# Four begun blocks at the scan's end, a sum of squares on TensorE and 1.1 convolution steps an item in a two-block model kernel

## Chip, cores and metric

One core of a Trainium2 chip runs the whole program. The metric is the device time of one execution in microseconds; the time before is the median of 3 runs.

## What is computed

The input x is 512 x 1024 (float32). A first block of two layers is followed by a second block of two mixers (cut from the reference; `rms_norm` divides by the root of the mean square):

```python
for l in range(2):                                   # first block
    hn = rms_norm(h, norm_mix_pre[l])
    y_attn, y_conv = dilated_attention(hn), short_conv(hn)
    o = gated_delta_rule(q, k, v, g, beta)           # scan over 8 chunks of 64
    y_gdn = rms_norm(o, norm_w) * silu(gate)
    mix = concatenate([y_attn, y_conv, y_gdn]) @ w_out[l]
    h = h + rms_norm(mix, norm_mix_post[l])
    xa = memory_cross_attention(rms_norm(h, norm_xattn_pre[l]), ...)
    h = h + rms_norm(xa, norm_xattn_post[l])
    f = swiglu_ffn(rms_norm(h, norm_ffn_pre[l]), w_gate_up[l], w_down[l])
    h = h + rms_norm(f, norm_ffn_post[l])
for i in range(2):                                   # second block: even, odd
    sh, sc, g = split(silu(c) @ mod_w[i] + mod_b[i])
    hl = rms_norm(x_lat, norm_g[i]) * (1 + sc) + sh
    x_lat = x_lat + g * mixer_i(hl, h_ctx)
return rms_norm(x_lat, final_g)
```

The even mixer attends over 256 context rows and the 512 rows; the odd one is a 31-tap depthwise convolution beside a neighbourhood attention of 8 heads.

## The kernel before

Activations lie transposed, as 8 chunks of 128 features x 512 positions. h is `hT`; a normalised input is held as a high and a low part (`xh`, `xl`). A weight block is 1024 x 128: `weight` loads it on SP's queue into `wr` (3 buffers), ACT casts it to the high part `wh` (L266) and DVE makes the low part `wl` (L267), 4 buffers each. Every product is three matmuls for each chunk, high by high, low by high, high by low (`mm3`, L293 to L295), summed in PSUM over 8 chunks, so a block is 24 matmuls of 128x512.

The order on each engine is set by a scheduler from the order in which the code issues, with some priorities; each engine then runs its rows in order. To fill TensorE, work is written as generators in `self.fill`, and `pump(n)` takes n steps of the first of them. `begin` starts blocks whose input is not ready as a whole, and `advance` adds the next chunk to each begun block as soon as that chunk of x exists (`gps` gives PSUM tile g for a block, `sps` a tile s for two).

Places that the change touches:
- `gdn_scan` (L834 to L872): the delta rule's scan over 8 chunks c. The begun blocks are the first two of `w_out` (g_2418 and g_2419 in the first layer); chunks 0 to 3 of their input are ready before the scan ends. At c = 7 four calls of `gdn_norm` follow, one for each quarter of the positions: the last O (L838, L855 and an add), its square, the scaling on DVE (L885), a transpose on PE (L888) and the gate. Then four `split` and `advance` (xh L399) bring chunks 4 to 7.
- `residual` (L409): R from the sum of squares (L378 the product with ones, then Ln L380 and Exp L381 on ACT), then for each chunk om x weight x R (L420) and the add into hT (L421). After the second layer's feed-forward, `colstat` forms hT's own sum of squares: squares on ACT (L392), seven adds on DVE (L393), one product with a matrix of ones (L378); then `modnorm` (L1341 to L1343) makes the even mixer's input, chunk by chunk, with three begun blocks.
- `ctx_stream` (L1450): the even mixer's work on the context rows, pumped as a filler through the second layer's feed-forward at RATES[1] = 1.1 steps a place, and on through the residual. Its matmuls are 128x256 (s<-ch,wh) and, at its end, for values of the odd mixer (L325 to L327).
- `odd` (L1671): 32 attention items; after the transposes of each, `steps(CR)` takes CR steps of the long convolution (`conv31`, L1795), each step one tap on DVE for each of four chunks (cu, R), 30 steps in all. DVE also masks and reduces for the softmax (L771, L768) and casts weights (L267). What is left of the convolution is run out when the last head begins (`start(3)`).

```python
        def steps(k):
            nonlocal n
            n += k
            while n >= 1:
                for c in conv:
                    next(c, None)
                n -= 1
```

Of the kernel before, what the change touches and what calls it, by code (L numbers as in the profile page):

```python
# [12 lines left out]
AF = mybir.ActivationFunctionType  # L13
# [4 lines left out]
D = 1024  # L18
S = 512
CTX = 256  # L20
MEM = 256
KC = D // 128
# [7 lines left out]
TS, TB = 2, 2  # L30
WP, XP = 1, 2
ER, OR = 1, (1.6, 2.1, 2.1, 1.7)
CR = 1.5
XOP = (0, 1)
RATES = (0.7, 1.1)
WR, WH, WL = 3, 4, 4
HA, HB, HD = 0, 0, 0
MP = (0, 0)
# [172 lines left out]
class Net:  # L211
# [128 lines left out]
    def begin(self, aps, extra=0):  # L340
# [7 lines left out]
        for i, ap in enumerate(aps):  # L348
            wh, wl = self.weight(ap)
            self.begun.append(((ap.tensor.name, ap.offset), wh, wl, ps[i]))  # L350

    def advance(self):
        c = self.nbegun
        self.nbegun += 1
        for _, wh, wl, ps in self.begun:
            self.mm3(ps, wh[:, c], wl[:, c], self.xh[:, c], self.xl[:, c], c == 0, c == KC - 1)


    def pump(self, n=1):
# [15 lines left out]
    def rsqrt_of(self, ss, out, scale, epscol, n=512, lhs=None):  # L375
        nc = self.nc
        ps = self.bps()[:, :n]
        nc.tensor.matmul(ps, self.ones if lhs is None else lhs, ss, start=True, stop=True)  # L378
        bias = 0.0 if epscol is None else self.epst[:, epscol:epscol + 1]
        nc.scalar.activation(out, ps, AF.Ln, bias=bias, scale=scale)  # L380
        nc.scalar.activation(out, out, AF.Exp, scale=-0.5)  # L381
        return ps

    def sumsq(self, acc, src, first, t=None):

# [20 lines left out]
        nc.scalar.copy(self.om[:, c], ps)  # L406
        self.sumsq(acc, ps, c == 0)

    def residual(self, acc, post, pre=None, R=None, scale=1.0 / D, epscol=0, chunk=2, aeps=0, keep=False):  # L409
        nc = self.nc  # L410
        Rp = self.R
        self.pump(2)
        with self.hp(HA):
            self.rsqrt_of(acc, Rp, 1.0 / D, aeps)
        self.pump(3)
        for c in range(KC):
            self.pump(chunk)
            t = self.tmp("rt")
            with self.hp(HB):
                nc.vector.scalar_tensor_tensor(t, self.om[:, c], self.sm(post, c), Rp, ALU.mult, ALU.mult)  # L420
                nc.vector.tensor_add(self.hT[:, c], self.hT[:, c], t)  # L421
                if pre is not None:
                    self.last = self.split(self.xh[:, c], self.xl[:, c], self.hT[:, c], self.sm(pre, c))
            if pre is not None:
                self.advance()
        if pre is not None:
            self.prestat(R, scale, epscol, keep)

    def prestat(self, R, scale=1.0 / D, epscol=0, keep=False):
        nc = self.nc  # L430
# [74 lines left out]
    def first(self, dbg=None):  # L505
# [5 lines left out]
        for l in range(2):  # L511
# [15 lines left out]
            else:  # L527
# [4 lines left out]
                with tc.tile_pool(name="ctx", bufs=1) as p:  # L532
                    self.fill = [self.ctx_stream(p)]
                    acc = self.xo_ffn(l, dbg, 1)
                    self.residual(acc, "f_post1", chunk=1, aeps=None)
                    if dbg and dbg(self, f"h3_{l}"): return
                    self.mark("ctxend")
                    R = self.colstat(self.hT, S, self.R)
                    self.pump(2)
                    self.begin([a["ev_in"][c] for c in (4, 0, 5)])  # L540
                    for _ in self.modnorm(0, 0, self.hT, self.xh, self.xl, S, R):
                        self.advance()
                        self.pump()
                    self.drain()
# [277 lines left out]
    def gdn_scan(self, l, p, heads):  # L822
# [3 lines left out]
        for c in range(8):  # L826
# [38 lines left out]
            if c == 7:  # L865
                while len(self.fill) > 3:
                    self.pump()
                for i in range(4):
                    self.gdn_norm(l, O, i, p)
        self.drain()  # L870
        self.mark(f"gdnend{l}")
        for h in range(4):  # L872
            self.split(self.xh[:, 4 + h], self.xl[:, 4 + h], self.om[:, 4 + h])
            self.advance()

    def gdn_norm(self, l, O, i, p):

# [971 lines left out]
```

## Time and profile before

| | |
|---|---|
| median of 3 runs | 2509.55 us (2506.88 to 2512.07) |
| the profiled execution's own time | 2508.96 us |
| its span, first to last instruction | 2507.2 us |
| mean granted TensorE clock | 0.986 |
| TensorE (PE) busy | 2409.2 us, 96% |
| weight loads (PEld) busy | 1960.1 us, 78% |
| VectorE (DVE) busy | 1755.7 us, 70% |
| ScalarE (ACT) busy | 1272.1 us, 51% |
| GpSimd (POOL) busy | 22.6 us, 1% |
| read from HBM | 240.83 MB, 98 GB/s over the span |

Times in the rows count from the span's start. A matmul's record is longer than its share of the engine, since matmuls are pipelined: what one costs is the distance from its start to the next start.

### The profile page before, as it was taken

What the parts mean: (1) busy time and instruction counts of PE and PEld (TensorE: products, weight loads), DVE (VectorE), ACT (ScalarE), POOL (GpSimd) and SP (SyncE); (2) the same over time, 40 slices, a digit from 0 to 9 for tenths busy, and PEclk for the clock granted to TensorE, in tenths of its full rate; (3) what the DMA queues carried; (4) which work ended last, traced back from release to release, by engine and by line L of the source; (5) the groups of instructions that cost most, each with busy time, mean ns of one, the idle gap of its engine ahead of it and who ended that gap; (6) DMA issues with size and microseconds to landing.
All of it is one profiled execution on the core that took longest, in us unless ns stands there. A gap on an engine that the chain in (4) does not pass through costs nothing.

```text
span 2507.2 us, 34818 instructions
## 1 busy us (share of the span) xinstructions
PE 2409.2 (96%) x13036; PEld 1960.1 (78%) x13036; DVE 1755.7 (70%) x3164; ACT 1272.1 (51%) x2371; POOL 22.6 (1%) x57
## 2 busy tenths in 40 slices
PE   8999899989999989998999999999998999999998
PEld 6678688768888766786887678888876888878787
DVE  7887675499984578876755755556566666669975
ACT  5754454444333447544545644445344666545584
POOL 0000000000000000000000000000000000000000
PEclk9999999999999999999999999999999999999999
DMA  5133133237753321331332233233335421333422
GB/s 180 51 86 77 51 118 126 93 115 238 214 174 109 97 83 51 86 77 51 125 120 78 83 97 97 93 100 127 118 116 155 119 64 56 115 101 99 115 77 68
DMA packets 96025, 263.30 MB, mean 105 GB/s; under 512 B 16232, under 2 KB 32232, under 8 KB 94704
## 3 DMA queue, kind: packets, MB, share of 16 engines
q1 hardware_dynamic: 92592, 257.72, 33.8%
q0 software_dynamic: 704, 2.17, 0.5%
q10 hardware_dynamic: 2560, 1.18, 0.3%
q8 instruction: 103, 1.69, 0.3%
q14 instruction: 66, 0.54, 0.1%
HBM read 240.83 MB, written 4.46 MB: 98 GB/s over the span
## 4 chain that ended last, share of the span: by engine, by line
PE 84%; DVE 9%; ACT 3%; DMA 2%; issue 2%; ACTq 0%; DVEq 0%; SPq 0%
PE g L293 19%; PE g L294 18%; PE g L295 18%; PE b L810 3%; PE s L293 3%; PE s L294 3%; PE s L295 3%; PE s L757 2%; PE b L1417 2%; PE b L378 2%; DVE wl L267 1%; DVE mj L1321 1%; PE b L797 1%; DMA mw<-in_mod_t_dram 1%; PE s L855 1%
## 5 line engine op out<-in xcount | busy, mean ns | idle before, releaser
L293 PE MATMUL g<-xh,wh 128*128 128x512 f32 (+1 forms) x1960 | 784.5, 402 | 40.1 <-ACT xh L400 9.1
L295 PE MATMUL g<-xh,wl 128*128 128x512 f32 (+1 forms) x1960 | 775.1, 396 | 6.0 <-DVE wl L267 5.9
L294 PE MATMUL g<-xl,wh 128*128 128x512 f32 (+1 forms) x1960 | 777.2, 397 | 0.0
L266 ACT CAST wh<-wr 128x1024 fp32r<-128x1024 f32 (+4 forms) x422 | 397.7, 945 | 632.5 <-PE g L294 492.7
L267 DVE TENSOR_TENSOR wl<-wr,wh 128x1024 fp32r<-128x1024 f32 (+4 forms) x422 | 458.4, 1089 | 162.6 <-ACT wh L266 156.5
L293 PEld LDWEIGHTS g<-xh,wh 128*128 128x128 f32 x1960 | 371.9, 190 | 128.1 <-ACT xh L400 12.1
L295 PEld LDWEIGHTS g<-xh,wl 128*128 128x128 f32 x1960 | 372.8, 190 | 85.5 <-DVE wl L267 8.0
L294 PEld LDWEIGHTS g<-xl,wh 128*128 128x128 f32 x1960 | 373.3, 190 | 76.0 <-issue 2.4
L293 PE MATMUL g<-yh,wh 128*128 128x512 f32 x352 | 139.8, 398 | 1.8 <-DVE om L1232 1.7
L294 PE MATMUL g<-yl,wh 128*128 128x512 f32 x352 | 138.1, 392 | 0.0
L295 PE MATMUL g<-yh,wl 128*128 128x512 f32 x352 | 137.9, 392 | 0.1
L1321 DVE CUSTOM_DVE_ANT_0 mj<-mw,csb 128x1024 f32<-128x1024 f32 x96 | 117.2, 1221 | 7.1 <-DMA mw<-in_mod_t_dram 6.0
L1232 DVE TENSOR_TENSOR om<-om,g 128x512 f32<-128x512 f32 x80 | 54.9, 686 | 63.6 <-PE g L295 63.2
L810 PE MATMUL b<-ident,P 128*128 128x128 f32 x608 | 96.0, 277 | 0.4 <-ACT P L783 0.3
L817 ACT COPY pt<-b 128x512 f32<-128x512 f32 (+3 forms) x136 | 71.6, 535 | 45.5 <-PE b L810 44.1
L468 ACT ACTIVATE rt<-rt 128x512 f32<-128x512 f32 x76 | 47.9, 631 | 91.6 <-DVE rt L467 90.5
L810 PEld LDWEIGHTS b<-ident,P 128*128 128x128 f32 x608 | 69.7, 141 | 24.0 <-ACT P L783 6.2
L454 DVE TENSOR_TENSOR fg<-g,R 128x512 f32<-128x512 f32 x42 | 29.0, 690 | 81.3 <-PE g L295 77.4
L783 ACT ACTIVATE P<-P,st 128x512 f32<-128x512 f32 (+4 forms) x96 | 65.9, 687 | 39.0 <-DVE st L779 16.7
L757 PE MATMUL s<-K,Q 128*128 128x256 f32 (+2 forms) x384 | 84.8, 338 | 0.0
L393 DVE TENSOR_TENSOR acc<-acc,sq 128x512 f32<-128x512 f32 (+1 forms) x111 | 75.6, 681 | 5.9 <-ACT sq L392 4.1
L293 PEld LDWEIGHTS g<-yh,wh 128*128 128x128 f32 x352 | 66.2, 188 | 17.1 <-issue 2.5
(444 smaller groups left out, 3899.8 us busy)
## 6 DMA issues: line engine op xcount, KB each, us to landing
wr<-in_w_gu_dram SPq DMA_DIRECT2D x88, 512.0 KB
wr<-in_w_in_dram SPq DMA_DIRECT2D x56, 512.0 KB
mw<-in_mod_t_dram SPq DMA_DIRECT2D x48, 512.0 KB
wr<-in_ev_in_dram SPq DMA_DIRECT2D x40, 512.0 KB
wr<-in_od_in_dram SPq DMA_DIRECT2D x32, 512.0 KB
wr<-in_w_down_dram SPq DMA_DIRECT2D x56, 192.0 KB
wr<-in_w_down_dram SPq DMA_DIRECT2D x24, 384.0 KB
wr<-in_w_out_dram SPq DMA_DIRECT2D x16, 512.0 KB
```

The lines of the kernel that those rows point to most:

```text
L266: nc.scalar.copy(hi[:, :k], raw[:, :k])
L267: nc.vector.tensor_sub(lo[:, :k], raw[:, :k], hi[:, :k].bitcast(F32))
L293: mm(ps, wh, xh, start=first, stop=False)
L294: mm(ps, wh, xl, start=False, stop=False)
L295: mm(ps, wl, xh, start=False, stop=last)
L393: nc.vector.tensor_add(acc, acc, t)
L757: self.nc.tensor.matmul(sp[:, c], q, K[u][:, k:k + c.stop - c.start], start=u == 0, stop=u == 1)
L783: nc.scalar.activation(P[:, c], src[i], AF.Exp, bias=shift, scale=-1.0 if neg else 1.0, accum_out=one(3 + i))
L810: nc.tensor.transpose(ps[:, 128 * (j % 4):128 * (j % 4) + 128], P, self.ident)
L817: nc.scalar.copy(out(j - m + 1, m), src)
L1232: nc.vector.tensor_add(self.om[:, c], self.om[:, c], ps)
L1321: nc.vector.tensor_tensor_reduce(out=junk, in0=raw, in1=csb[:, b], scale=1.0, scalar=0.0, op0=ALU.mult, op1=ALU.add, accum_out=self.mod[i] ...
```

## The change

Four edits.
1. In `gdn_scan`, at c = 7, a generator `begin_more` joins the fillers: it begins blocks 2 and 3 of `w_out` in one tile s and issues their chunks 0 to 3. Behind the scan chunks 4 and 5 are split and advanced, 6 and 7 split alone, and `finish` adds what is left to each of the four blocks. Both layers.
2. `residual` has a flag `stat`, set for f_post1 alone: each chunk of hT is squared on ACT as soon as it is added, and a product with the ones adds it up in PSUM (L451, 8 products). `colstat`, with its seven adds, is gone there; `rsqrt_end` is the Ln and Exp alone.
3. RATES[1] goes from 1.1 to 1.07.
4. CR goes from 1.5 to 1.1.

```diff
--- before.py
+++ after.py
@@ -30,9 +30,9 @@
 TS, TB = 2, 2
 WP, XP = 1, 2
 ER, OR = 1, (1.6, 2.1, 2.1, 1.7)
-CR = 1.5
+CR = 1.1
 XOP = (0, 1)
-RATES = (0.7, 1.1)
+RATES = (0.7, 1.07)
 WR, WH, WL = 3, 4, 4
 HA, HB, HD = 0, 0, 0
 MP = (0, 0)
@@ -349,11 +349,30 @@
             wh, wl = self.weight(ap)
             self.begun.append(((ap.tensor.name, ap.offset), wh, wl, ps[i]))
 
+    def begin_more(self, aps):
+
+        p = self.sps()
+        for i, ap in enumerate(aps):
+            wh, wl = self.weight(ap)
+            ps = p[:, 512 * i:512 * i + 512]
+            self.begun.append(((ap.tensor.name, ap.offset), wh, wl, ps))
+            for c in range(self.nbegun):
+                self.mm3(ps, wh[:, c], wl[:, c], self.xh[:, c], self.xl[:, c], c == 0, False)
+                if c % 2:
+                    yield
+
     def advance(self):
         c = self.nbegun
         self.nbegun += 1
         for _, wh, wl, ps in self.begun:
             self.mm3(ps, wh[:, c], wl[:, c], self.xh[:, c], self.xl[:, c], c == 0, c == KC - 1)
+
+    def finish(self):
+
+        for _, wh, wl, ps in self.begun:
+            for c in range(self.nbegun, KC):
+                self.mm3(ps, wh[:, c], wl[:, c], self.xh[:, c], self.xl[:, c], c == 0, c == KC - 1)
+        self.nbegun = KC
 
 
     def pump(self, n=1):
@@ -376,10 +395,14 @@
         nc = self.nc
         ps = self.bps()[:, :n]
         nc.tensor.matmul(ps, self.ones if lhs is None else lhs, ss, start=True, stop=True)
+        self.rsqrt_end(ps, out, scale, epscol)
+        return ps
+
+    def rsqrt_end(self, ps, out, scale, epscol):
+        nc = self.nc
         bias = 0.0 if epscol is None else self.epst[:, epscol:epscol + 1]
         nc.scalar.activation(out, ps, AF.Ln, bias=bias, scale=scale)
         nc.scalar.activation(out, out, AF.Exp, scale=-0.5)
-        return ps
 
     def sumsq(self, acc, src, first, t=None):
 
@@ -406,7 +429,8 @@
         nc.scalar.copy(self.om[:, c], ps)
         self.sumsq(acc, ps, c == 0)
 
-    def residual(self, acc, post, pre=None, R=None, scale=1.0 / D, epscol=0, chunk=2, aeps=0, keep=False):
+    def residual(self, acc, post, pre=None, R=None, scale=1.0 / D, epscol=0, chunk=2, aeps=0, keep=False, stat=False):
+
         nc = self.nc
         Rp = self.R
         self.pump(2)
@@ -419,12 +443,19 @@
             with self.hp(HB):
                 nc.vector.scalar_tensor_tensor(t, self.om[:, c], self.sm(post, c), Rp, ALU.mult, ALU.mult)
                 nc.vector.tensor_add(self.hT[:, c], self.hT[:, c], t)
+                if stat:
+                    sq = self.tmp("sq")
+                    nc.scalar.activation(sq, self.hT[:, c], AF.Square)
+                    if c == 0:
+                        ps = self.bps()
+                    nc.tensor.matmul(ps, self.ones, sq, start=c == 0, stop=c == KC - 1)
                 if pre is not None:
                     self.last = self.split(self.xh[:, c], self.xl[:, c], self.hT[:, c], self.sm(pre, c))
             if pre is not None:
                 self.advance()
         if pre is not None:
             self.prestat(R, scale, epscol, keep)
+        return ps if stat else None
 
     def prestat(self, R, scale=1.0 / D, epscol=0, keep=False):
         nc = self.nc
@@ -532,10 +563,11 @@
                 with tc.tile_pool(name="ctx", bufs=1) as p:
                     self.fill = [self.ctx_stream(p)]
                     acc = self.xo_ffn(l, dbg, 1)
-                    self.residual(acc, "f_post1", chunk=1, aeps=None)
+                    ps = self.residual(acc, "f_post1", chunk=1, aeps=None, stat=True)
                     if dbg and dbg(self, f"h3_{l}"): return
                     self.mark("ctxend")
-                    R = self.colstat(self.hT, S, self.R)
+                    R = self.R
+                    self.rsqrt_end(ps, R, 1.0 / D, 0)
                     self.pump(2)
                     self.begin([a["ev_in"][c] for c in (4, 0, 5)])
                     for _ in self.modnorm(0, 0, self.hT, self.xh, self.xl, S, R):
@@ -865,13 +897,16 @@
             if c == 7:
                 while len(self.fill) > 3:
                     self.pump()
+                self.fill.append(self.begin_more([a["w_out"][l][c] for c in (2, 3)]))
                 for i in range(4):
                     self.gdn_norm(l, O, i, p)
         self.drain()
         self.mark(f"gdnend{l}")
         for h in range(4):
             self.split(self.xh[:, 4 + h], self.xl[:, 4 + h], self.om[:, 4 + h])
-            self.advance()
+            if h < 2:
+                self.advance()
+        self.finish()
 
     def gdn_norm(self, l, O, i, p):
 
```

On PE at the end of the first layer's scan, from its last transposes (b<-ident,O) to the begun blocks (g_2418, g_2419), there stood before:

```order
L888 MATMUL b_2474<-ident,O_2041 128x128 x4
L855 MATMUL s_2402<-vn_2403,at_1050 64x128
L855 MATMUL s_2402<-vn_2403,at_1055 64x128
L855 MATMUL s_2402<-vn_2403,at_1060 64x128
L855 MATMUL s_2402<-vn_2403,at_1065 64x128
L888 MATMUL b_2493<-ident,O_2041 128x128 x4
L888 MATMUL b_2512<-ident,O_2041 128x128 x4
L293 MATMUL g_2418<-xh,wh_2422 128x512
L293 MATMUL g_2419<-xh,wh_2428 128x512
L294 MATMUL g_2418<-xl,wh_2422 128x512
```

and now, with s_2545 the tile of blocks 2 and 3 (line 923 was 888, 887 was 855):

```order
L887 MATMUL s_2402<-vn_2403,at_1065 64x128
L294 MATMUL s_2545<-xl,wh_2548 128x512
L295 MATMUL s_2545<-xh,wl_2549 128x512
L293 MATMUL s_2545<-xh,wh_2548 128x512
L294 MATMUL s_2545<-xl,wh_2548 128x512
L295 MATMUL s_2545<-xh,wl_2549 128x512
L293 MATMUL s_2545<-xh,wh_2566 128x512
L294 MATMUL s_2545<-xl,wh_2566 128x512
L923 MATMUL b_2493<-ident,O_2041 128x128 x4
L295 MATMUL s_2545<-xh,wl_2567 128x512
L293 MATMUL s_2545<-xh,wh_2566 128x512
L294 MATMUL s_2545<-xl,wh_2566 128x512
```

Between those small products, and ahead of the first matmul of g_2418, 24 matmuls into s_2545 now stand, in groups of 7, 7, 8 and 2; before, blocks 2 and 3 (g_2631, g_2670) followed behind g_2418 and g_2419.

On DVE at the end of the second layer's feed-forward residual there stood before, from the last multiply and adds into hT on, with acc the sum of hT's squares:

```order
L420 SCALAR_TENSOR_TENSOR rt_15786<-om,small,R 128x512
L420 SCALAR_TENSOR_TENSOR rt_15795<-om,small,R 128x512
L421 TENSOR_TENSOR hT<-hT,rt_15786 128x512
L421 TENSOR_TENSOR hT<-hT,rt_15795 128x512
L393 TENSOR_TENSOR acc_1545_15798<-acc_1545_15798,sq_15800 128x512
L267 TENSOR_TENSOR wl_15828<-wr_15825,wh_15827 128x1024
L393 TENSOR_TENSOR acc_1545_15798<-acc_1545_15798,sq_15803 128x512
L267 TENSOR_TENSOR wl_15850<-wr_15847,wh_15849 128x1024
L393 TENSOR_TENSOR acc_1545_15798<-acc_1545_15798,sq_15806 128x512
L267 TENSOR_TENSOR wl_15856<-wr_15853,wh_15855 128x1024
```

and now (line 444 was 420, 445 was 421, 422 was 399):

```order
L267 TENSOR_TENSOR wl_15752<-wr_15749,wh_15751 128x1024
L422 TENSOR_TENSOR Kcl_15694<-s_15656,Kch_15693 128x256
L444 SCALAR_TENSOR_TENSOR rt_15761<-om,small,R 128x512
L444 SCALAR_TENSOR_TENSOR rt_15773<-om,small,R 128x512
L445 TENSOR_TENSOR hT<-hT,rt_15761 128x512
L445 TENSOR_TENSOR hT<-hT,rt_15773 128x512
L267 TENSOR_TENSOR wl_15782<-wr_15779,wh_15781 128x1024
L422 TENSOR_TENSOR Kcl_15743<-s_15705,Kch_15742 128x256
L444 SCALAR_TENSOR_TENSOR rt_15791<-om,small,R 128x512
L267 TENSOR_TENSOR wl_15808<-wr_15805,wh_15807 128x1024
L445 TENSOR_TENSOR hT<-hT,rt_15791 128x512
L267 TENSOR_TENSOR wl_15823<-wr_15820,wh_15822 128x1024
```

The seven adds into acc are gone, and the weight casts (L267) that stood between them stand between the adds into hT. PE has a product L451 for each chunk, between the matmuls on context.

On DVE in the odd mixer, this ended the stretch of 47 rows ahead of the cast of wl_20233, with om the convolution's sum:

```order
L1795 SCALAR_TENSOR_TENSOR om<-R,small,om 128x503
L1795 SCALAR_TENSOR_TENSOR om<-cu_19137,small,om 128x503
L471 TENSOR_TENSOR sq_20170<-rt_20168,sq_20170 128x512
L1795 SCALAR_TENSOR_TENSOR om<-cu_19206,small,om 128x503
L1406 TENSOR_TENSOR om<-om,sq_20170 128x512
L1795 SCALAR_TENSOR_TENSOR om<-cu_19275,small,om 128x503
L771 ISA P_20223,st_20222<-s_20200,rpb_20194 128x512
L771 ISA st_20222 128x1
L768 TENSOR_REDUCE st_20222<-s_20200 128x1
L267 TENSOR_TENSOR wl_20233<-wr_20230,wh_20232 128x1024
```

and this now ends the stretch of 29 rows ahead of the same block's cast, wl_20203 (line 1830 was 1795, 803 was 771):

```order
L1830 SCALAR_TENSOR_TENSOR om<-R,small,om 128x510
L1830 SCALAR_TENSOR_TENSOR om<-cu_19135,small,om 128x510
L1830 SCALAR_TENSOR_TENSOR om<-cu_19204,small,om 128x510
L803 ISA P_19894,st_19856<-s_19875,rpb_19705 128x512
L803 ISA st_19856 128x1
L800 TENSOR_REDUCE st_19856<-s_19875 128x1
L1830 SCALAR_TENSOR_TENSOR om<-cu_19273,small,om 128x510
L809 TENSOR_SCALAR st_19856<-st_19856 128x1
L267 TENSOR_TENSOR wl_20203<-wr_20200,wh_20202 128x1024
```

Of the 47 rows 20 are taps of the convolution, of the 29 now 12. Ahead of the cast at the last head (wl_20781) 69 rows now stand behind the cast before it, 28 of them taps.

## Rows read from the trace of the kernel before

**Rows 1.** The page: busy time by engine, and the chain that ended last.

```profile
PE 2409.2 (96%) x13036; PEld 1960.1 (78%) x13036; DVE 1755.7 (70%) x3164; ACT 1272.1 (51%) x2371; POOL 22.6 (1%) x57
...
PE 84%; DVE 9%; ACT 3%; DMA 2%; issue 2%; ACTq 0%; DVEq 0%; SPq 0%
```

**Rows 2.** Busy time by stretch: length, PE, PEld, DVE, ACT, POOL, granted clock, DMA share, GB/s.

```profile
250.00:300.00 50.00, 43.06 (x256) 33.39 (x253) 31.61 (x87) 19.18 (x66) 0.00 (x0) 0.90 0.09 32
...
1450.00:1850.00 400.00, 400.00 (x2122) 333.76 (x2121) 220.32 (x374) 179.13 (x335) 0.00 (x0) 1.00 0.33 105
...
1850.00:1900.00 50.00, 41.87 (x217) 33.37 (x216) 46.35 (x75) 29.17 (x47) 0.00 (x0) 1.00 0.52 157
...
2300.00:2350.00 50.00, 50.00 (x364) 41.73 (x363) 48.81 (x106) 31.71 (x75) 0.00 (x0) 1.00 0.53 143
```

**Rows 3.** PE's timeline, end of the first layer's scan: start, length, instruction, [idle before <-releaser].

```profile
285.32 1.08 PE L855 MATMUL s<-vn,at 64*64 64x128 f32 x8 [1.24 <-ACT O L838]
...
287.93 0.88 PE L888 MATMUL b<-ident,O 128*128 128x128 f32 x4 [1.53 <-DVE O L885]
...
290.47 1.09 PE L888 MATMUL b<-ident,O 128*128 128x128 f32 x4 [1.66 <-DVE O L885]
...
293.17 1.22 PE L293 MATMUL g<-xh,wh 128*128 128x512 f32 x2 [1.62 <-ACT xh L399]
...
307.66 0.59 PE L293 MATMUL g<-xh,wh 128*128 128x512 f32 x1
```

**Rows 4.** PE's timeline, end of the second layer's scan.

```profile
1169.27 1.22 PE L293 MATMUL g<-xh,wh 128*128 128x512 f32 x2 [1.62 <-ACT xh L399]
...
1182.73 0.59 PE L293 MATMUL g<-xh,wh 128*128 128x512 f32 x1
...
1188.40 0.39 PE L293 MATMUL g<-xh,wh 128*128 128x512 f32 x1
```

**Rows 5.** PE's timeline, the second layer's last residual and the even mixer's start.

```profile
1874.47 1.02 PE L378 MATMUL b<-acc,ones 128*128 128x512 f32 x2
...
1890.52 0.50 PE L326 MATMUL s<-wl,ch 128*128 128x512 f32 x1 [1.39 <-DVE wl L267]
...
1894.79 0.50 PE L326 MATMUL s<-wl,ch 128*128 128x512 f32 x1 [1.26 <-DVE wl L267]
...
1902.30 1.74 PE L378 MATMUL b<-acc,ones 128*128 128x512 f32 x2 [4.71 <-DVE acc L393]
...
1907.02 1.22 PE L293 MATMUL g<-xh,wh 128*128 128x512 f32 x2 [2.98 <-ACT xh L1342]
...
1912.73 0.49 PE L294 MATMUL g<-xl,wh 128*128 128x512 f32 x1
...
1926.43 1.12 PE L378 MATMUL b<-sq,blk 128*128 128x512 f32 x2
```

**Rows 6.** The same stretch on DVE and on ACT.

```profile
1891.72 1.28 DVE L421 TENSOR_TENSOR hT<-hT,rt 128x512 f32<-128x512 f32 x2
...
1893.52 1.21 DVE L267 TENSOR_TENSOR wl<-wr,wh 128x1024 fp32r<-128x1024 f32 x1
...
1893.70 0.63 ACT L392 ACTIVATE sq<-hT 128x512 f32<-128x512 f32 x1 [2.53 <-DVE acc L393]
...
1904.08 0.69 ACT L380 ACTIVATE R<-b,epst 128x512 f32<-128x512 f32 x1 [2.49 <-PE b L378]
```

**Rows 7.** The odd mixer, DVE's timeline and then PE's.

```profile
2331.53 1.22 DVE L267 TENSOR_TENSOR wl<-wr,wh 128x1024 fp32r<-128x1024 f32 x1
...
2354.99 1.21 DVE L267 TENSOR_TENSOR wl<-wr,wh 128x1024 fp32r<-128x1024 f32 x1
...
2356.89 2.04 DVE L1795 SCALAR_TENSOR_TENSOR om<-cu,small,om 128x502 f32<-128x502 f32 x3
...
2356.25 0.50 PE L295 MATMUL g<-xh,wl 128*128 128x512 f32 x1 [4.12 <-DVE wl L267]
...
2359.93 0.46 PE L295 MATMUL g<-xh,wl 128*128 128x512 f32 x1
```

## Prediction

> **What bounds the kernel.** I read the page first: TensorE (PE) is busy 2409.2 of the 2507.2 us span, DVE 70%, ACT 51%, and the chain that ended last is 84% PE and 9% DVE [rows 1]. So time leaves in two ways only: PE does less, or one of its holes closes. The table by stage says where holes are. In the first block's second feed-forward part PE is busy for the whole 400.00 us from 1450 to 1850: nothing can be won there. At the end of the first layer's scan it has 43.06 of 50 at a granted clock of 0.90, in 1850 to 1900 only 41.87, while DVE has 46.35 [rows 2]. In 2300 to 2350 PE is full, but so is DVE (48.81) [rows 2]: a DVE instruction that comes late there finds no slack.
>
> Then the holes, in PE's order of time. At the scan's end PE waits four times (1.24, 1.53, 1.66, 1.62 us) in a chain in which ACT and DVE finish the last heads; the first two after it show 1.22 us for the pair [rows 3], which is the 1.2 GHz level and fits the window's granted 0.90. At the 2.4 GHz level they stand 0.23 apart: 24 in 5.67 us from 1182.73 to 1188.40 [rows 4]. Around the end of that feed-forward part PE stands 4.71 us for DVE's last sum of squares, runs the product with ones, stands 2.98 us for the normalised input, and then runs at the slow spacing until 1912.73 [rows 5]. In the last stage it stands 4.12 us for a weight's low half (wl) that DVE makes, then runs slowly until 2359.93, nine matmuls in 3.7 us, 0.41 apart [rows 7].
>
> **1. Four begun blocks in the scan, both layers.** Removed nothing; 24 matmuls (two blocks, chunks 0 to 3) move from behind the scan to between its last products; the order's rows show them in four groups of 7, 7, 8 and 2. Their weights' casts stand at the same places on ACT and DVE, so no other engine gets work. PE's holes there add up to 1.24+1.53+1.66+1.62 = 6.05 us [rows 3], the 24 matmuls are 24 x 0.23 = 5.5 us, so they fit. PE runs in order: where a group is a little longer than its hole, the next small product, and the chain behind it, starts late; I take 0.7 us in all (0.3 to 1.0). After the chain 48 matmuls remain (four blocks, chunks 4 to 7), 11.0 us if the clock stays high, and a ones-product of some 0.45. So the next block starts at 293.17+0.7+11.0+0.45 = 305.3. Before, it started at 307.66+5.67 = 313.3 [rows 3, 4]: **-8.0**. Second layer: 1169.27+0.7+11.0+0.45 = 1181.4 against 1188.40 [rows 4]: **-7.0** (its restart was shorter before: 13.46 us from the chain's end to the last block's start, 14.49 in the first layer [rows 3, 4]). Without any gain in clock it is 5.5 minus at most 1 for the delay, so -4.5 each; with no delay -8.7 and -7.7.
>
> **2. Sum of squares on TensorE, with 3. the slower pump (1.1 to 1.07).** The pump moves some 32 matmuls of 256 columns from ahead of the ffn's last sum (the 1874.47 row) to behind it; counted in the order, 92 in place of 60 stand between that sum and the first begun block. Ahead of it PE is full [rows 2], so the sum comes 32 x 0.115 = 3.7 us earlier. Behind it, before: 1907.02-1874.47 = 32.55 us to the first begun matmul, 51.96 to the end of that begin [rows 5]. After, PE's own work: the sum 1.0, 92 x 0.115 = 10.6, 32 matmuls x 0.23 = 7.4, eight ones-products x 1.0 = 8.0 (the 1.02 of the 1874.47 row [rows 5]): 27.0. Then 88 matmuls (72 and 16 moved behind) x 0.23 = 20.2, in all 47.2.
>
> DVE loses seven adds, of the length of the hT adds (1.28 for two [rows 6]), but the casts that stood between them now stand between the hT adds. From the sum: 2.7 us until R is there (the product 1.0, Ln and Exp 0.7 each as in [rows 6], some 0.3 between them), 16 multiplies and adds at 0.65, four small casts of a quarter of a weight cast's elements (0.35 each, an estimate from the 1.21 us of one [rows 6]), seven weight casts at 1.14 (1.21 less the overlap of neighbours): 22.5. Then a square 0.63 [rows 6] and the last product 1.0, and Ln, Exp, one DVE and one ACT step, 3.0: the first begun matmul at 27 to 28.3. DVE sets the pace by about a microsecond; 14 of the 32 matmuls stand behind the last ones-product and cover that last chain, so no cold restart. On SP's queue this stretch's last context-value weight now stands behind the three weights of the begun blocks; the DMA engines are at 0.52 there [rows 2], so I cost that at nothing; were it late, those 14 matmuls would wait for it. 48.5-51.96 = -3.5, and -3.7 from the pump: **-7**. Bounds: the holes that can go are 1.39+1.26+4.71+2.98 = 10.3, the slow restart 13 x 0.2 = 2.6 and the ones-product's 0.7 (1.74 for 1.02) [rows 5], 13.6 in all, less 7 added products (7.0): -6.6 behind the sum, -10.3 with the pump. At the other end PE keeps its holes and gives back behind the sum what came earlier: 0.
>
> A rule speaks against this part. The rows show PE idle 8.1 of 50 us here and DVE busy 46.35 [rows 2], so work taken from DVE should count, and work put on PE should fall into holes. Were PE the bound of this stretch throughout, the seven products would come on top: +7.0 in place of -7 (rival F). The Trainium skill, in Perfetto Trace Analysis (Identifying the Most-Contended Engine), has it that the engine with the highest occupancy is the one to relieve first, which over the whole span is PE, and this edit loads it. The same page (Optimization Strategy) adds that the engine can change between regimes; this case's window agrees, with 41.87 on PE and 46.35 on DVE. I go by the row.
>
> **4. Convolution steps 1.5 to 1.1 an item.** No work changes; 120 long-convolution rows spread over more items. The late cast at 2354.99 stood behind DVE's queue: from the cast before it (2331.53) 23.5 us, 47 rows, 20 of them convolution at about 0.66 each (three in 2.04, overlapping) [rows 7]. After, 29 rows, 12 of them convolution, stand between the two. PE's order moves by only a few rows there, so the cast should be in time, and the 4.12 us and nine slow matmuls x 0.2 = 1.8 go: at best -5.9. The casts behind it were in time but close (PE came to them soon after they ended), and the convolution that is left is done in a burst: 69 rows, 28 of them convolution, stand ahead of the cast at the last head. I take **-5**; the other end is a new wait there (rival D).
>
> **Sum.** -8-7-7-5 = -27; 2508.96-27 = **2482**. The median of the runs, 2509.55, lies 0.6 above the profiled execution, so no shift.
>
> **Rivals.**
> A, the forecast: 2482, chance 0.60.
> B, part 2 gains nothing: DVE's casts, now ahead of the hT adds, hold each ones-product as the adds held the one before. For it: DVE has only 3.65 us free of 50. Against: seven adds of 0.6 are gone. 2489. 0.12.
> C, the clock does not recover at the scan's end: the moved matmuls run 0.42 apart, 10.1 us where 6.05 are free, 4 lost a layer. For it: clock 0.90 in that window. Against: the rows are slow only after 293.17, behind four holes, and the holes are what is filled. 2482+8 = 2490. 0.08.
> D, the burst: the cast at the last head is late. From the cast before it DVE has 28 x 0.66 = 18.5 us of convolution and some 11 of other rows, PE some 14 in that stretch (its rows of the order at their lengths in the trace): 15 at worst, less the lead that DVE has by then. Middle 2490, worst 2497. 0.12.
> E, the slower side: with the pump at 1.07 each of the 28 context weights used inside the feed-forward part is reached out of step with DVE's cast, and each makes PE wait as at 1894.79 (1.26 us) [rows 5]: 28 x 1.26 = 35, 2517. It decides from 22 such waits on (22 x 1.26 = 27.7, more than the 27 gained). Against: eight windows without a hole, DVE at half load there. 0.04.
> F, PE bounds the stretch of part 2 throughout, and the products come on top: 2482+14 = 2496. For it: PE's 96% of the span [rows 1]. Against: its 8.1 idle us there. 0.04.
> That the change does not do what it says is excluded by the order: the groups, the eight products and the sparser convolution all stand there.
>
> **Numbers.** The range 2473 to 2497: below, 8.7+7.7+10.3+5.9 = 32.6 us would be 2476, and 3 for holes that close further down; above, B, C, F and D's worst. E and what is below are left out. A alone: 2476 to 2487. A measurement of this kernel tells about 0.2%, 5 us, from no change (the runs differ by 5). Faster by more than that: A, B, C, D but for a little, F: 0.93. Same: 0.03; slower: 0.04.
>
> **What would show it.** Right: at both scan ends matmuls into a fourth and third block between the last products, no holes over 0.5 us but the last, matmuls at 0.23 from 293 on, the next block some 8 and 7 us earlier relative to the scan; no add from line 393's kind in the last feed-forward residual and no stretch of PE idle over 3 us around it; no 4 us wait for wl near 2356, and none over 3 us at the last head. Wrong: new wl waits in 1450 to 1850, ones-products each waiting for a square by more than 1 us, a clock below 0.95 in the window of the scan's end, or a wl wait of 5 us or more behind the burst.

## The result and the profile after

The changed kernel takes 2479.07 us (median of 4 runs, 2476.74 to 2483.35) against 2509.54: a ratio of 0.9881, 95% interval 0.9864 to 0.9898, so 30 us less. Its profiled execution has a span of 2476.6 us, 30.6 shorter than before. The page, busy time by engine and the chain that ended last:

```profile
PE 2401.9 (97%) x13050; PEld 1956.0 (79%) x13050; DVE 1751.4 (71%) x3157; ACT 1271.2 (51%) x2371; POOL 22.6 (1%) x57
...
PE 88%; DVE 7%; ACT 3%; DMA 2%; issue 1%; SPq 0%; ACTq 0%; DVEq 0%
```

PE is busy 7.3 us less, although 14 more records stand in its row; that fits matmuls that ran at the 1.2 GHz level before and are shorter now. DVE's share of the chain fell from 9 to 7%. By stretch (columns as in [rows 2]; the chain of the scan's end begins only 1.6 us earlier than before, so the first stretch stands where it stood; at the other two places the program is 19 and 24 us earlier, and these stretches are moved by 20):

```profile
250.00:300.00 50.00, 47.96 (x284) 37.85 (x284) 32.70 (x87) 21.02 (x70) 0.00 (x0) 1.00 0.10 32
...
1430.00:1830.00 400.00, 400.00 (x2130) 334.19 (x2129) 221.87 (x375) 179.49 (x338) 0.00 (x0) 1.00 0.34 105
1830.00:1880.00 50.00, 47.72 (x229) 36.80 (x229) 45.74 (x73) 32.21 (x52) 0.00 (x0) 0.97 0.52 156
```

PE has 47.96 of 50 at the scan's end where it had 43.06, the clock 1.00 for 0.90; 47.72 for 41.87 at the feed-forward's end, the clock 0.97 for 1.00; and the 400 us between are as full as before. Where the time came from is read best from products that both kernels have. The lengths below run from the start of one such product to the next in the profiled executions (the scan's end: from the last product of vn and kd to the sum of squares of the w_out product):

| stretch | before | after | difference |
|---|---|---|---|
| scan's end, first layer | 58.62 | 49.71 | -8.9 |
| scan's end, second layer | 57.34 | 49.68 | -7.7 |
| feed-forward of the second layer, to its sum of squares | 466.75 | 461.80 | -4.9 |
| that sum to the sum ahead of the odd mixer | 333.44 | 331.05 | -2.4 |
| odd mixer, to the last two sums | 287.42 | 283.44 | -4.0 |
| all the rest | | | -2.7 |

The rest was not forecast. It is 1.6 us ahead of the first scan's end and 1.1 between the two scans, in code that the change leaves alone. The traces of the eleven runs below have the same code there: they come to the last product of vn and kd in the first layer between 278.5 and 280.6 us (before 280.8, after 279.2), and take 816.2 to 820.5 us between the scans (817.7 and 816.7). So it is of the size by which executions differ. The same traces tell how far the rows of the table can be trusted, wherever the code of a stretch is that of the changed kernel: its scan's end takes 49.7 us in each, the way to the feed-forward's sum 460.2 to 461.8, the stretch behind that sum 330.3 to 332.7 and the odd mixer 281.5 to 283.7. Before, each stretch is known from one trace alone.

### The profile page after: what moved, and what is told of

Read it like the earlier page. It is cut to its first block, busy times and chain, and to the rows that moved or that the text cites. A ratio compares the mean times of both kernels' runs of the same rounds, so it can differ in the third digit from the quotient of the medians.

```text
span 2476.6 us, 34843 instructions
## 1 busy us (share of the span) xinstructions
PE 2401.9 (97%) x13050; PEld 1956.0 (79%) x13050; DVE 1751.4 (71%) x3157; ACT 1271.2 (51%) x2371; POOL 22.6 (1%) x57
## 4 chain that ended last, share of the span: by engine, by line
PE 88%; DVE 7%; ACT 3%; DMA 2%; issue 1%; SPq 0%; ACTq 0%; DVEq 0%
PE g L293 19%; PE g L294 19%; PE g L295 19%; PE s L293 4%; PE s L294 3%; PE s L295 3%; PE b L842 3%; PE s L789 3%; PE b L1452 2%; PE b L397 2%; PE b L829 1%; DVE wl L267 1%; PE s L327 1%; PE s L325 1%; PE s L326 1%
## 5 line engine op out<-in xcount | busy, mean ns | idle before, releaser
L293 PE MATMUL g<-xh,wh 128*128 128x512 f32 (+1 forms) x1928 | 766.8, 399 | 35.7 <-ACT xh L423 9.1
L294 PE MATMUL g<-xl,wh 128*128 128x512 f32 (+1 forms) x1928 | 760.6, 395 | 0.5 <-DVE xl L422 0.5
L295 PE MATMUL g<-xh,wl 128*128 128x512 f32 (+1 forms) x1928 | 757.4, 393 | 1.9 <-DVE wl L267 1.8
L267 DVE TENSOR_TENSOR wl<-wr,wh 128x1024 fp32r<-128x1024 f32 (+4 forms) x422 | 458.7, 1089 | 144.8 <-ACT wh L266 137.5
L293 PEld LDWEIGHTS g<-xh,wh 128*128 128x128 f32 x1928 | 363.3, 189 | 121.5 <-ACT xh L423 12.9
L295 PEld LDWEIGHTS g<-xh,wl 128*128 128x128 f32 x1928 | 364.2, 189 | 78.0 <-DVE wl L267 3.4
L294 PEld LDWEIGHTS g<-xl,wh 128*128 128x128 f32 x1928 | 364.5, 189 | 74.3 <-issue 2.4
L295 PEld LDWEIGHTS g<-yh,wl 128*128 128x128 f32 x352 | 66.1, 188 | 15.1
```

The lines of the kernel that those rows point to most:

```text
L267: nc.vector.tensor_sub(lo[:, :k], raw[:, :k], hi[:, :k].bitcast(F32))
L293: mm(ps, wh, xh, start=first, stop=False)
L294: mm(ps, wh, xl, start=False, stop=False)
L295: mm(ps, wl, xh, start=False, stop=last)
```

## Experiments

Each kernel is the changed one with the edit shown. Medians carry an interval of about 4 us on either side, so smaller terms are read from the traces.

### Two begun blocks again

```diff
-                self.fill.append(self.begin_more([a["w_out"][l][c] for c in (2, 3)]))
...
-            if h < 2:
-                self.advance()
-        self.finish()
+            self.advance()
```

> The changed kernel with the scan's end as before: two begun blocks, nothing between the last small products. Theory (the holes of the scan's end are filled and the clock stays at its high level): both scan ends lose what the trace showed them to gain, 9.1 and 8.0 us, so 2479 + 17 = 2496, with the four holes of 1.2 to 1.7 us and the slow matmuls behind them back in both layers. Rival (only the 24 moved matmuls count, 5.5 us each; the rest of the two gains was chance in where the clock fell): 2490.

2495.23 us (ratio to before 0.9950, 0.9934 to 0.9966): 16 more than the changed kernel, the theory's 17. Both scan's ends are back at 58.63 and 58.09. PE's timeline (start, length, instruction, idle time before and its releaser) of this kernel at the end of the first chain, and of the changed kernel:

```profile
290.27 1.09 PE L920 MATMUL b<-ident,O 128*128 128x128 f32 x4 [1.66 <-DVE O L917]
292.97 1.22 PE L293 MATMUL g<-xh,wh 128*128 128x512 f32 x2 [1.62 <-ACT xh L422]
```

```profile
289.03 0.60 PE L923 MATMUL b<-ident,O 128*128 128x128 f32 x4
...
291.25 0.74 PE L293 MATMUL g<-xh,wh 128*128 128x512 f32 x2 [1.15 <-ACT xh L422]
...
302.33 0.59 PE L397 MATMUL b<-macc,ones 128*128 128x256 f32 x2
302.57 0.59 PE L293 MATMUL g<-xh,wh 128*128 128x512 f32 x1
```

Of the four holes of [rows 3] one of 1.15 us is left. The four transposes take 0.60 in place of 1.09 us, the first pair 0.74 in place of 1.22: with the holes filled the clock is at its high level there.

### Other matmuls in the holes

Two begun blocks, and in the holes 24 matmuls on their weights into a tile that nothing reads.

```diff
-                self.fill.append(self.begin_more([a["w_out"][l][c] for c in (2, 3)]))
+                self.fill.append(self.dummy())
...
-            if h < 2:
-                self.advance()
-        self.finish()
+            self.advance()
...
+    def dummy(self):
+        p = self.sps()
+        for i in range(2):
+            _, wh, wl, _ = self.begun[i]
+            for c in range(self.nbegun):
+                self.mm3(p[:, 512 * i:512 * i + 512], wh[:, c], wl[:, c], self.xh[:, c], self.xl[:, c], c == 0, c == self.nbegun - 1)
+                if c % 2:
+                    yield
```

> The changed kernel with two begun blocks as before, and in the place of the moved matmuls 24 others on the weights of those two blocks, whose sum nothing reads: work is added (2 x 24 matmuls), none is moved. It tells the clock's share of the gain at the scan's end from the moved work's. Theory (the holes let the clock fall; filled, the matmuls behind them run 0.23 apart at once): against the run with two begun blocks alone (2495) 2.5 us are won in the first layer and 1.2 in the second, less 0.3 to 1.0 each that the small products come later: 2493, and no matmul over 0.5 us behind the scan. Rival (the clock falls by the scan's small products themselves, or the restart is chance): the slow matmuls stay, 2495 to 2498.

2495.46 us (0.9942, 0.9927 to 0.9957): the medians of this kernel and of the one before cannot be told apart. In the traces the scan's ends can: 56.16 and 56.19 us in place of 58.63 and 58.09, so 48 added matmuls make the two stretches shorter by 2.5 and 1.9 us. The first matmuls behind the chain:

```profile
292.25 0.74 PE L293 MATMUL g<-xh,wh 128*128 128x512 f32 x2 [1.15 <-ACT xh L432]
292.97 0.50 PE L294 MATMUL g<-xl,wh 128*128 128x512 f32 x1
293.31 0.40 PE L295 MATMUL g<-xh,wl 128*128 128x512 f32 x1
```

None is slow. So the gain of 8.9 and 7.7 is two things. The clock gives 2.5 us in the first layer, and in the second 1.2 against the kernel before (57.34) or 1.9 against the one with two begun blocks (58.09). The moved work gives 6.5 us (56.16 to 49.71): 24 matmuls, 5.5, a wait of 0.49 us for acc that stood between the blocks, and some 0.5 us that is not accounted for. That the whole execution shows nothing of the 4.4 us is not explained by this stretch; against that kernel the same trace loses 2.6 us between the sums at 531 and 879 (its granted clock is 0.93 in 525 to 550, the other's 1.00) and 2.4 behind the feed-forward's sum.

### Seven adds on DVE behind the residual again

```diff
-                    ps = self.residual(acc, "f_post1", chunk=1, aeps=None, stat=True)
+                    self.residual(acc, "f_post1", chunk=1, aeps=None)
...
-                    R = self.R
-                    self.rsqrt_end(ps, R, 1.0 / D, 0)
+                    R = self.colstat(self.hT, S, self.R)
```

> The changed kernel with the sum of squares behind the last feed-forward residual on DVE again (seven adds, one product with ones), the pump left at 1.07. Theory (DVE sets the pace there and PE's holes took the seven added products): the holes for the sum and for the normalised input come back, some 4.7 + 3.0 us, with a slow restart of 2.6 and a slow product of 0.7, less the 7.0 us of products: 2479 + 4 = 2483, at most 2486. Rival (PE bounds the stretch, and the gain seen there is the pump's): 2479 - 7 = 2472 to 2479.

2483.49 us (0.9902, 0.9888 to 0.9917), the theory's 2483. From the feed-forward's sum to the odd mixer's it takes 4.4 us longer than the changed kernel. The holes come back, in other places than in [rows 5]; PE's timeline, then ACT's and DVE's:

```profile
1875.06 0.50 PE L326 MATMUL s<-wl,ch 128*128 128x512 f32 x1 [1.45 <-DVE wl L267]
1882.28 0.51 PE L325 MATMUL s<-wh,ch 128*128 128x512 f32 x1 [4.42 <-ACT wh L266]
1882.62 1.83 PE L397 MATMUL b<-acc,ones 128*128 128x512 f32 x2
...
1881.18 1.04 ACT L266 CAST wh<-wr 128x1024 fp32r<-128x1024 f32 x1 [1.22 <-DMA wr<-in_od_v_dram]
...
1880.93 0.69 DVE L416 TENSOR_TENSOR acc<-acc,sq 128x512 f32<-128x512 f32 x1
```

The wait of 4.42 us is put down to a late weight and not to the sum. SP issues the load of that weight at 1876.81 us, after the cast on DVE (1875.52, 1.22 us long) that this queue waited for, ACT's cast waits 1.22 us for it to land, and PE stands for the cast. But the last add into acc ends on DVE only at 1881.62, so without the late weight the sum would have been held almost as long, 0.7 us less. Both ways begin at DVE.

In the changed kernel the same stretch has no wait but the one of the sum itself:

```profile
1850.24 2.05 PE L397 MATMUL b<-acc,ones 128*128 128x512 f32 x2 [1.84 <-DVE acc L416]
1858.06 1.02 PE L451 MATMUL b<-sq,ones 128*128 128x512 f32 x2
...
1873.93 1.02 PE L451 MATMUL b<-sq,ones 128*128 128x512 f32 x2
...
1878.10 0.74 PE L293 MATMUL g<-xh,wh 128*128 128x512 f32 x2
...
1898.46 1.12 PE L397 MATMUL b<-sq,blk 128*128 128x512 f32 x2
```

### The squares chunk by chunk, on DVE

```diff
-                    sq = self.tmp("sq")
-                    nc.scalar.activation(sq, self.hT[:, c], AF.Square)
-                    if c == 0:
-                        ps = self.bps()
-                    nc.tensor.matmul(ps, self.ones, sq, start=c == 0, stop=c == KC - 1)
+                    if c == 0:
+                        ps = self.tmp("acc2", bufs=1)
+                    self.sumsq(ps, self.hT[:, c], c == 0)
...
-                    self.rsqrt_end(ps, R, 1.0 / D, 0)
+                    self.rsqrt_of(ps, R, 1.0 / D, 0)
```

> The changed kernel with the sum of squares behind the last feed-forward residual formed chunk by chunk beside the adds into hT, as now, but on DVE: seven adds and one product in place of eight products on PE. It tells the earlier start of the squares from the move to TensorE. Theory (DVE sets the pace there): seven adds of 0.6 to 0.68 us go on DVE's path, some 4.5, and PE's seven products, 7.0, come off a PE that waits: 2479 + 3 = 2482, between the changed kernel and the one with seven adds behind the residual (2483.5). Rival (it was only the order, squares begun earlier; TensorE's part costs PE 7 us for nothing): 2474 to 2477.

2485.40 us (0.9906, 0.9892 to 0.9921): not better than the adds behind the residual, and 6 more than on PE, by the medians and also in the traces between the feed-forward's start and the odd mixer's sum. With the adds between the hT adds, DVE comes to the weights later, and PE waits for a wl:

```profile
1876.27 0.50 PE L326 MATMUL s<-wl,ch 128*128 128x512 f32 x1 [3.71 <-DVE wl L267]
```

So the earlier start of the squares is not what was won; the seven adds taken from DVE are. It also answers the rule that the prediction weighed: PE, the busiest engine over the span (by its matmuls' 96% and by its weight loads' 78%, against DVE's 70%), has 7 us more of products in the changed kernel, and the stretch is shorter.

### The same edit ahead of the odd mixer

```diff
+            if i == 0:
+                sq = self.tmp("sq")
+                nc.scalar.activation(sq, self.hT[:, c], AF.Square)
+                if c == 0:
+                    self.ostat = self.bps()
+                nc.tensor.matmul(self.ostat, self.ones, sq, start=c == 0, stop=c == KC - 1)
...
-        R = self.colstat(self.hT, S)
+        R = self.tmp("Rp", bufs=1)
+        self.rsqrt_end(self.ostat, R, 1.0 / D, 0)
```

> The changed kernel with the same edit at another place: the sum of squares ahead of the odd mixer as eight products with ones, one behind each block of the even mixer's last product, in place of seven adds on DVE and one product. Theory (it pays only where PE has holes): PE is full through that product, so the seven added products cost 7 us, and from the 2.86 us wait for the sum only one add, some 0.7, and perhaps a slow product's 1.0 come back: 2479 + 5.5 = 2484.5. Rival (a shorter last chain counts most, as at the feed-forward's end): 2476 to 2479.

2486.83 us (0.9907, 0.9893 to 0.9922), 8 more than the changed kernel by the medians. The profiled execution is the fastest of its runs (2482.59), and from the second layer's feed-forward to the last two sums its trace is 4.4 us longer. So the edit that gains at one place loses at the other, somewhere between 4 and 8 us. PE's timeline:

```profile
2173.17 1.12 PE L1705 MATMUL b<-sq,ones 128*128 128x512 f32 x2
...
2186.36 1.13 PE L1705 MATMUL b<-sq,ones 128*128 128x512 f32 x2 [1.57 <-ACT sq L1702]
2190.47 1.22 PE L293 MATMUL g<-xh,wh 128*128 128x512 f32 x2 [2.98 <-ACT xh L1377]
```

Seven products stand in a full row, one behind each block; only the last wait became shorter, 1.57 for 2.86 us, and the 2.98 stays.

### The pump at 1.1 again

```diff
-RATES = (0.7, 1.07)
+RATES = (0.7, 1.1)
```

> The changed kernel with the pump of the context work at 1.1 steps again. Theory (the pump moves 3.7 us of matmuls behind the feed-forward's sum, but the sum then waits 1.84 us and runs 1.0 us longer at the low clock): undoing it costs 3.7 - 2.9 = about 1: 2480, with no wait of that sum. Rival (the pump is half of the gain there): 2483 to 2486.

2481.30 us (0.9894, 0.9877 to 0.9910): 2 more, within the intervals. In the trace the feed-forward's sum comes 6.4 us later, with no wait, and the stretch behind it is 5.1 us shorter: 1.4 in favour of 1.07. With the adds left on DVE the slower pump gains 2.9 us over the same two stretches (797.3 us in the kernel with seven adds behind the residual, 800.2 before). Traces of unchanged code spread there from 790.6 to 794.4 us, so neither gain stands clear of that.

The expectation's 1.0 us for a sum at the low clock is no cost of its own. In the repeat of the changed kernel the sum is short, but then PE waits for a wl:

```profile
1850.14 1.10 PE L397 MATMUL b<-acc,ones 128*128 128x512 f32 x2 [2.18 <-DVE acc L416]
1851.98 0.58 PE L295 MATMUL s<-ch,wl 128*128 128x256 f32 x1 [0.74 <-DVE wl L267]
```

In both executions the product behind the sum starts 1.84 us after it.

### 1.5 convolution steps an item again

```diff
-CR = 1.1
+CR = 1.5
```

> The changed kernel with 1.5 convolution steps an item again. Theory (a weight's low half was late behind the convolution's taps on DVE): one wait of about 4 us of PE for wl returns in the odd stage, with nine or so slow matmuls behind it: 2479 + 5 = 2484. Rival (the order of DVE does not matter, the wait was chance): no wl wait over 1 us, 2479.

2485.07 us (0.9910, 0.9895 to 0.9925), 6 more by the medians. Not all of that is the pace: the trace is 6.4 us longer, 3.1 of it in the odd mixer and 3.8 between the two scans, where the code is the same. Counted from the odd mixer's first begun matmul on, past a sum whose length varies with the clock (1.10 to 2.05 us), the difference is 4.0. DVE's timeline and PE's at the wait that returns:

```profile
2331.07 1.21 DVE L267 TENSOR_TENSOR wl<-wr,wh 128x1024 fp32r<-128x1024 f32 x1
...
2332.33 0.68 PE L295 MATMUL g<-xh,wl 128*128 128x512 f32 x1 [3.96 <-DVE wl L267]
2332.81 0.63 PE L293 MATMUL g<-xh,wh 128*128 128x512 f32 x1
```

The same block's cast in the changed kernel, and the product that needs it:

```profile
2300.84 1.22 DVE L267 TENSOR_TENSOR wl<-wr,wh 128x1024 fp32r<-128x1024 f32 x1
...
2324.79 0.39 PE L295 MATMUL g<-xh,wl 128*128 128x512 f32 x1
```

DVE ends that cast 23 us ahead of PE's need. From here to the last head the margins of the casts are 22.7, 24.4, 26.1, 19.4 and 1.1 us; at 1.5 steps they are 0.1, 0.2, 0.8, 1.5 and 13.4, the last one when the convolution is over. So the pace sets when DVE's lead is spent: early, where four casts then find 1.5 us or less of it, one of them too little, or in the burst at the last head, where one finds 1.1.

### 0.9 steps an item

```diff
-CR = 1.1
+CR = 0.9
```

> The changed kernel with 0.9 convolution steps an item in place of 1.1. Ahead of the last head 21 steps are then done in place of 25 or 26, and 8 or 9 in place of 5 are run out there in one go: some 34 taps, 22 us of DVE. Theory (the burst is harmless as long as DVE's lead covers it, and that lead is some 10 to 20 us): a wait for wl of 3 to 8 us appears at the last head: 2479 + 5 = 2484. Rival (the pace does not matter once no cast stands behind 20 taps): 2479, no wait over 1 us.

2481.73 us (0.9893, 0.9876 to 0.9909), and PE waits for no wl in the odd stage. The stall that the theory expected did not come: the casts ahead have leads of 28 to 32 us, and the cast at the last head again has 1.1 us to spare. DVE's timeline and PE's first product on that cast, with 1.1 steps and then with 0.9:

```profile
2339.24 0.69 DVE L803 CUSTOM_DVE_ANT_0 P<-s,rpb 128x512 f32<-128x512 f32 x1 [0.40 <-PE s L789]
...
2365.14 1.22 DVE L267 TENSOR_TENSOR wl<-wr,wh 128x1024 fp32r<-128x1024 f32 x1
...
2367.49 0.39 PE L295 MATMUL g<-xh,wl 128*128 128x512 f32 x1
```

```profile
2336.91 0.69 DVE L803 CUSTOM_DVE_ANT_0 P<-s,rpb 128x512 f32<-128x512 f32 x1 [0.39 <-PE s L789]
...
2362.79 1.22 DVE L267 TENSOR_TENSOR wl<-wr,wh 128x1024 fp32r<-128x1024 f32 x1
...
2365.14 0.39 PE L295 MATMUL g<-xh,wl 128*128 128x512 f32 x1
```

In both kernels DVE has caught up with PE at the first of these rows and has waited for it, and from that wait to the cast it runs 23 taps in 25.9 us. The 35 taps of this run, against 28, are those since the cast before, which stands further ahead; the additional ones lie ahead of the wait. So this run put the same load behind the wait and not a larger one, and what a larger one there would cost stays open. The odd mixer is 1.9 us shorter than in the changed kernel's trace, but another trace with 1.1 steps is as short (281.5 us both).

### The context values at the odd mixer's start

Two kernels that try to win more: 48 matmuls that do not depend on h leave the stretch behind the feed-forward's sum for the holes at the odd mixer's start. The edit is that of the first; the second leaves RATES as it is. Beside them stands a repeat of the changed kernel that differs from it in nothing.

```diff
+FA, FB = 3, 3
...
-RATES = (0.7, 1.07)
+RATES = (0.7, 1.02)
...
-        yield from self.gemm_tok(a["od_v"][0], x, lambda ps: nc.scalar.copy(self.dv, ps))
+        for u in range(2):
+            nc.sync.dma_start(self.cx[u], x[u].bitcast(F32))
...
+        self.fill = [self.gemm_tok(a["od_v"][0], x, lambda ps: nc.scalar.copy(self.dv, ps))]
+        acc = self.tmp("acc2", bufs=1)
+        for c in range(KC):
+            self.sumsq(acc, self.hT[:, c], c == 0)
+        self.pump(FA)
+        self.rsqrt_of(acc, R, 1.0 / D, 0)
+        self.pump(FB)
```

> The changed kernel once more, word for word, timed in the same rounds as the two kernels that follow: 2479, within 3 us. Its profile shows how far the terms read from one execution move from one execution to the next: the two scan ends, the feed-forward's end and the odd stage should each give the same within 1 us, and larger differences stand where the clock happened to fall.

> Not part of the change: the context values of the odd mixer (48 matmuls, 10.9 us, independent of h) leave the stretch behind the feed-forward's sum, and their input, kept in device memory meanwhile, is loaded again; 18 of them stand ahead of the product with ones at the odd mixer's start, 18 behind it. So that the first stretch keeps its cover, the pump goes from 1.07 to 1.02. Theory (what was won at the scan's end can be won wherever independent matmuls are at hand): the holes at the odd mixer's start, 2.86 and 2.98 us, and the slow restart, some 2.6, go, 8.4 in all, less what reopens in the first stretch: 2479 - 6 = 2473. Rival (four more weight casts on DVE, 4.6 us, and four on ACT stand in the same chain that PE waits for, and 2 MB more to load): the holes move but stay, 2477 to 2482.

> As the run before, with the pump left at 1.07. Theory (behind the feed-forward's sum PE needs those matmuls as cover, since DVE sets the pace there): holes reopen there, 2 to 4 us, so 2475 to 2477, slower than with 1.02. Rival (DVE is relieved of four casts there, 4.6 us, and keeps up): the same as with 1.02 or faster, 2472 to 2473.

The repeat takes 2480.05 us (2476.36 to 2482.53), the two others 2479.00 and 2478.04 (their ratios to before 0.9888, 0.9873 to 0.9903, and 0.9879, 0.9863 to 0.9896): no difference that can be told. The repeat's scan's ends are 49.69 and 49.68 us, its odd mixer within 0.1 of the first trace, the stretch between the two sums 1.2 longer. In the kernel with the pump at 1.07 the holes at the odd mixer's start are gone; busy time in 2180 to 2200 there:

```profile
2180.00:2200.00 20.00, 20.00 (x89) 16.09 (x88) 13.93 (x19) 9.66 (x14) 0.00 (x0) 1.00 0.22 79
```

PE's wait that it has instead, behind the feed-forward's sum:

```profile
1876.95 0.79 PE L294 MATMUL g<-xh,wh 128*128 128x512 f32 x2 [3.18 <-ACT xh L1381]
```

In the changed kernel 15.73 of the 20 us from 2180 are busy, at a granted clock of 0.74. With the pump at 1.02 other waits open at the same place, as the context's own normalisation falls into it:

```profile
1848.05 0.67 PE L398 MATMUL b<-cx,ones 128*128 128x256 f32 x2 [2.43 <-DVE cx L417]
1851.54 0.80 PE L294 MATMUL s<-ch,wh 128*128 128x256 f32 x2 [2.82 <-ACT ch L1381]
```

At the odd mixer's sum the two kernels are 3.6 and 3.4 us ahead of the changed one, with 30 of the 48 matmuls, 6.8 us, still to do; from the second layer's feed-forward to the last two sums they take 1076.4 and 1075.3 us, the changed kernel and its repeat 1076.3 and 1077.1. Both the theory's 2473 and its step from 1.07 to 1.02 fell. Read with the waits above, the matmuls that cover one chain are missed where they covered another; these kernels also load 2 MB more and cast four weights elsewhere, and no run separates the two. Neither version beats the changed kernel by anything measured.

## Why the prediction was right

- **Scan's end, -8.0 and -7.0.** Measured -8.9 and -7.7 in the traces, and 16 us together by the medians when undone. The mechanism is as told: the four groups stand in the holes, 48 matmuls follow at 0.23. Mis-sized was the delay of the chain, taken as +0.7: from the last vn,kd product to the first begun matmul it was 12.38 and 12.13 us before and is 12.08 now, no loss, since the small products in the chain run at the high clock (the last four transposes 0.60 us for 1.09). Rival C, the clock that does not recover, is out: 1.00 in the window, and the added matmuls alone bring it there. The prediction's opening names two ways only in which time leaves, less work and closed holes; its own sums use the third, the same matmuls at the higher clock, 1.2 to 2.5 us a layer here.
- **Sum of squares and pump, -7.** Measured -4.9 ahead of the sum and -2.4 behind it, -7.3. The parts lie differently: the sum comes 4.9 us earlier and not 3.7, although it now waits 1.84 us for DVE's add, which was not foreseen. Mis-sized is the pump's term: against the run with 1.1 steps the sum comes 6.4 us earlier, and 1.5 of that is hidden in the comparison with before, whose trace ran the first matmuls of this stretch faster (10.4 us to the first one on the new input, 11.9 after, 11.9 with 1.1 steps). From its start to the first begun matmul it is 27.86 us (27 to 28.3 forecast; 29.88 in the repeat), to the end of the begin 48.22 (48.5). The step that DVE sets the pace holds, and the two runs with DVE's adds show it; that it is by a microsecond is not shown. The load that was costed at nothing cost nothing here, but the same weight was late in the kernel with the adds on DVE behind the residual. Rivals B and F are out by the runs with adds on DVE: PE's products are paid from holes here, and not ahead of the odd mixer. That the total came out within 0.3 us of the forecast is in part luck: the pump and the wait were both missed, and traces of the same code spread by 3.8 us over these two stretches.
- **Convolution, -5.** Measured -4.0 in the trace; from the first begun matmul on -4.9, since the sum at the odd mixer's start ran 2.04 us here and 1.10 before. Undone, it is 4.0 counted so, and 6 by the medians. The wait for wl and its slow matmuls are gone. Rival D, the burst, stayed away by 1.1 us: that is the lead of the cast at the last head. The prediction subtracted "the lead that DVE has by then" without a number, so nothing in it told this end from the other, and that it went well is partly luck.
- **Rival E** did not happen: the 400 us are full.
- **The sum.** -8.9-7.7-7.3-4.0 = -27.9 against -27 forecast. The other 2.7 us of the profiled execution's span stand in stretches with unchanged code and are of the size of the differences between executions; that they are chance was not shown. The three parts were each undone by themselves, and each gave back its share; only the pump's own share is not clear of the spread.

## What to carry to other kernels

Read a window for which engine is full before moving work between engines: the same seven products gained 4 us where PE had holes and lost 4 to 8 where it had none. Independent matmuls in the holes of a latency chain pay twice, for themselves and for the clock, but they are a stock: those taken for one chain are missing in another. For an engine that runs in order, look at its lead at each point where another needs it, not at its busy share; slowing a filler kept a lead of 20 us that had been spent too early.

## What was not expected of the hardware

Added work can shorten a stretch: 24 matmuls with no use, in holes of 1.2 to 1.7 us, made both scan's ends shorter by 2.5 and 1.9 us than without them, since four transposes in the chain took 0.60 in place of 1.09 us and the matmuls behind stood 0.23 and not 0.42 apart. And with the holes filled the stretch became the same from run to run: 49.68 to 49.73 us in both layers of nine kernels, where the unfilled one took 57.34 to 58.63.
